# First norm and first projection of a hybrid encoder step: GpSimd's share moved to VectorE, smaller token tiles, a half-block projection loop and another queue for the first weights

## The chip, the core and the metric

The kernel runs on one core of a Trainium2 chip, in one launch. The metric is the device time of that launch in microseconds (us). The kernel before was timed three times: 3157.12, 3160.59 and 3160.79 us, a median of 3160.59 us.

## The reference

One layer of a streaming encoder works on a prompt of 2048 tokens and on a sample of 32 tokens, each token a vector of 1024 channels, in float32. The layer has an attention branch, a gated linear attention branch (GLA), a merge, and a gated MLP with a short convolution. The change sits in its very first lines:

```python
def rmsnorm(x, g):
    xf = x.astype(jnp.float32)
    r = lax.rsqrt(jnp.mean(xf * xf, axis=-1, keepdims=True) + EPS)
    return (xf * r).astype(x.dtype) * g
...
    shift_m, scale_m, gate_m, shift_f, scale_f, gate_f = adaln_modulation(c, p['w_ada'], p['b_ada'])

    h = rmsnorm(x, p['g_pre_mix']) * (1.0 + scale_m) + shift_m
    z = h @ p['w_in']
```

Here `adaln_modulation` is a small product of the conditioning vector with `w_ada`. The matrix `w_in` has 5136 columns. The part that matters here makes `h` for all 2080 tokens and the 512 columns of `z` that hold GLA's queries ("Q") and keys ("K").

## The kernel before

**Layout.** Channels lie on the partitions: the 1024 channels are 8 chunks of 128 (index `k`), and tokens run along the free axis. The 2080 tokens are 5 blocks of 416 (`NB`), and each block is two half blocks of 208 (`NH`), numbered 0 to 9. Each float32 operand of a large product is split into a high and a low part of type float32r. A product then takes three matmuls (`mm3`, L78 to L80): high by high, high by low, low by high. `h` lives in `hA` (blocks 0 to 3) and `hB` (block 4), a high and a low tile each.

**The steps of the first norm**, for one half block `hb`:

- `prep_load` (L263): two DMAs (L267) on the queue of SyncE (SP), each bringing a tile of 4 chunks by 208 tokens. Six such tiles exist, three half blocks' worth.
- `prep_stats` (L270): ScalarE squares two chunks at a time (L276, L279), and another engine adds the squares up (L280, L281). The adding engine is VectorE for half blocks 0 and 1 and GpSimd for 2 to 9. One buffer holds the squares that wait to be added.
- `rstd_bcast` (L140): the sums are split (L69 on ScalarE, L72 on VectorE). TensorE adds them over the partitions with a matrix of ones (L148, L149). ScalarE takes logarithm and exponential (L154, L155), and VectorE polishes the result in three dependent steps (L156 to L158). This is the reciprocal root `r`, on all partitions.
- `prep_apply` (L290), per chunk: VectorE multiplies by `r` and the scale (L299), ScalarE adds the shift and rounds to the high part (L300), VectorE takes the low part (L301). Half block 2 is an exception: for its odd chunks GpSimd does the multiplications (L288, L297).

**The conditioning** (`ada_load` L305, `ada` L314): 8 small products whose weights come in DMAs of 256 KB (L310) through six buffers, again on SP's queue. The scale and shift of two chunks are ready after a second set of tiny matmuls (L327) and VectorE's L134 and L138.

**The projection** (`wave` L341): 4 column chunks of 128 (two of Q, two of K) each accumulate over the 8 chunks `k` in a PSUM bank. One step of `k` is 4 x 3 = 12 matmuls of 416 columns, and one block is 96 matmuls. Its weights are loaded in pieces (`w_pieces`, L180): a DMA of 256 KB on SP's queue (L187) into one of two raw buffers, ScalarE's rounding (L191), VectorE's low part (L192). After a block, `t_evac` (L202) copies the banks out, Q on ScalarE (L230) and K on VectorE (L233), and stores them (L235).

**Order.** TensorE's instructions run in the order of the program text. The instructions of the other engines, and SP's DMAs, are reordered at build time by a list scheduler that follows data dependences and the text's order as priority; on the chip each queue then runs strictly in the built order. Block 0 is written out by hand (L353 to L418), interleaved with the conditioning. Blocks 1 to 4 are the loop at L422 over `s_` = 2 to 9. Two values of `s_` make one block: the first takes `k` = 0 to 3 of all 416 tokens, the second `k` = 4 to 7. In step `s_` the kernel loads half block `s_` + 4, takes statistics of `s_` + 3, and finishes and applies the norm of `s_` + 2. In block 4 the two steps are Q's chunks and K's chunks instead.

**PSUM.** Of 8 banks, `psx` (tag `px`) has 6 and `psm` (tag `pm`) has 2. The waves, the conditioning and the norm's sums all use `px` here.

**After it** comes `n_tile`, the projection of the other columns, which starts as soon as block 4 is done.

Of the kernel before, what the change touches and what calls it, by code (L numbers as in the profile page):

```python
# [10 lines left out]
F32 = mybir.dt.float32  # L11
# [3 lines left out]
OP = mybir.AluOpType  # L15
# [43 lines left out]
def encoder_step(ctx: ExitStack, tc: tile.TileContext, I, O):  # L59
# [120 lines left out]
    def w_pieces(wp, c0, n, w, kp, wr=2):  # L180

        hi = wp.tile([128, KD, w], F32R, name="wh", tag="wh")
        lo = wp.tile([128, KD, w], F32R, name="wl", tag="wl")

        def piece(kk):
            raw = wp.tile([128, kp, w], F32, name="wr", tag="wr", bufs=wr)
            d = nc.sync.dma_start(raw[:, :, :n], dap(w_in, kk * 128 * WIN + c0, [[WIN, 128], [128 * WIN, kp], [1, n]]))  # L187
            if behind.pop():
                tc.keep_in_program_order(d)
            behind.append(False)  # L190
            nc.scalar.activation(hi[:, kk:kk + kp, :n], raw[:, :, :n], AF.Copy)  # L191
            nc.vector.tensor_sub(lo[:, kk:kk + kp, :n], raw[:, :, :n], f32(hi[:, kk:kk + kp, :n]))  # L192

        return (hi, lo), [lambda kk=kk: piece(kk) for kk in range(0, KD, kp)]
# [48 lines left out]
    with ExitStack() as st:  # L243
# [17 lines left out]
        POOL = {2: (1, 3, 5, 7)}  # L261

        def prep_load(hb, q_=nc.sync):  # L263
            XK[hb] = []
            for k in range(0, KD, 4):
                x = pp.tile([128, 4, NH], F32, name="xk", tag="xk", bufs=6)
                q_.dma_start(x, dap(I["xT"], k * 128 * T + NH * hb, [[T, 128], [128 * T, 4], [1, NH]]))  # L267
                XK[hb].append(x)

        def prep_stats(hb, add):  # L270

            sq = pp.tile([128, 2, NH], F32, name="sq", tag="sq", bufs=2)
            for k in range(0, KD, 2):
                x = XK[hb][k // 4][:, k % 4:k % 4 + 2]
                if k == 0:
                    nc.scalar.activation(sq, x, AF.Square)  # L276
                    continue
                s2 = pp.tile([128, 2, NH], F32, name="sq2", tag="sq2")
                nc.scalar.activation(s2, x, AF.Square)  # L279
                add.tensor_add(sq, sq, s2)  # L280
            add.tensor_add(sq[:, 0], sq[:, 0], sq[:, 1])  # L281
            return lambda: rstd_bcast(pp, psx, "px", sq[:, 0], NH, NH, 2)

        def prep_scale(hb):
            for k in POOL.get(hb, ()):
                for a, e, s in parts(NH * hb, NH):
                    xs = XK[hb][k // 4][:, k % 4, a:e]
                    nc.gpsimd.tensor_scalar(xs, xs, mod[:, 1, k, s:s + 1], 1.0, op0=OP.mult, op1=OP.mult)  # L288

        def prep_apply(hb, r, ks_=range(KD)):  # L290
            for k in ks_:
                for a, e, s in parts(NH * hb, NH):
                    hi, lo = [h_at(x, k, NH * hb + a, e - a) for x in range(2)]
                    xs = XK[hb][k // 4][:, k % 4, a:e]
                    s1, s2 = mod[:, 1, k, s:s + 1], mod[:, 0, k, s:s + 1]
                    if k in POOL.get(hb, ()):
                        nc.gpsimd.tensor_mul(xs, xs, r[:, a:e])  # L297
                    else:
                        nc.vector.scalar_tensor_tensor(xs, xs, s1, r[:, a:e], op0=OP.mult, op1=OP.mult)  # L299
# [39 lines left out]
        w0, steps = zip(*[w_pieces(wp, c0, 256, 272, 2, 2) for _, c0 in first])  # L339

        def wave(b, ks_, ps, chunks=range(4)):  # L341
            for k in ks_:
                for i in chunks:
                    mm3(ps[i][:, :NB], [t_terms(w0[i // 2], 128 * (i % 2), b, k)], first=k == 0, last=k == KD - 1)
# [8 lines left out]
        fin0 = prep_stats(0, nc.vector)()  # L353
# [6 lines left out]
        fin1 = prep_stats(1, nc.vector)()  # L360
# [8 lines left out]
        prep_load(2)  # L369
# [6 lines left out]
        prep_load(3)  # L376
# [5 lines left out]
        fins[2] = prep_stats(2, nc.gpsimd)  # L382
# [5 lines left out]
        prep_load(4)  # L388
# [5 lines left out]
        fins[3] = prep_stats(3, nc.gpsimd)  # L394
# [7 lines left out]
        prep_scale(2)  # L402
        m1 = ada(3, 0)
        r2 = fins.pop(2)()()
# [4 lines left out]
        prep_apply(2, r2)  # L409
        prep_load(5)  # L410
        wave(0, (5, ), ps)
        f3 = fins.pop(3)()
        wave(0, (6, ), ps)
        r3 = f3()
        wave(0, (7, ), ps)
        prep_apply(3, r3)
        fins[4] = prep_stats(4, nc.gpsimd)
# [1919 lines left out]
```

## Time and profile before

| what | before |
|---|---|
| median of three timed runs | 3160.59 us |
| the profiled execution, its own time | 3162.02 us |
| its span (first to last instruction) | 3160.3 us |
| first matmul of the projection of block 0 starts at | 27.21 us |
| block 1 starts at | 71.25 us |
| block 2 starts at | 97.36 us |
| block 3 starts at | 121.72 us |
| block 4 starts at | 145.75 us |
| the next stage's first matmul (`n_tile`) starts at | 163.85 us |

A row of the timeline reads: start, duration, engine, line, operation, output <- inputs, shapes, count, and in brackets the idle time before it with what released it. PE is TensorE, PEld its weight load, DVE VectorE, ACT ScalarE, POOL GpSimd, SP the queue of SyncE. Matmuls are pipelined, so the spacing of their starts tells the rate, not their durations. A row of the waits reads: who waited, for whom, total us, times, longest. A row of groups reads: line, engine, operation, tiles and shapes, count, busy us, mean ns, and the idle time before with its releasers. Stretches list, per engine, busy us and number of instructions.

### The profile page before, as it was taken

The numbers are of one execution on the slowest core, as the hardware profiler recorded it, in microseconds if no ns is written. First come the engines' busy times: TensorE is split into PE (matmuls) and PEld (weight loads), VectorE is DVE, ScalarE is ACT, GpSimd is POOL, SyncE is SP. The second block draws the span as 40 slices with busy tenths as digits, with TensorE's granted clock in tenths as the row PEclk, the third lists the DMA queues.
The fourth block names the chain that finished last, engine by engine and source line by source line (L and its number), as shares of the span: only waits on it lengthen the run. The fifth ranks groups of instructions, "written<-read, shape, count | busy, mean of one in ns | idle before, by whom it ended". The sixth has DMA issues, their size and how long they took to land. (4 is left out here: it accounts for less than half of the span.)

```text
span 3160.3 us, 56426 instructions
## 1 busy us (share of the span) xinstructions
PE 3047.7 (96%) x19748; PEld 2947.7 (93%) x19748; DVE 2239.8 (71%) x4879; ACT 1648.8 (52%) x3792; POOL 269.4 (9%) x427
## 2 busy tenths in 40 slices
PE   6999999999999999999999999999999999999997
PEld 4899999998999999988999899999999999999997
DVE  6735617774555555566677799998888778897877
ACT  4522224443555555544454655567666556576755
POOL 2201201112111111120000000000000000000001
PEclk9999999999999999999999999999999999999998
DMA  7354435554433334575457686788897667888784
GB/s 220 91 156 125 139 98 142 137 137 128 130 109 111 107 100 117 169 230 184 140 175 227 211 256 210 223 256 225 249 265 217 189 189 230 263 250 284 242 267 146
DMA packets 598478, 580.12 MB, mean 184 GB/s; under 512 B 53201, under 2 KB 526530, under 8 KB 598194
## 3 DMA queue, kind: packets, MB, share of 16 engines
q1 hardware_dynamic: 553026, 527.86, 56.2%
q10 hardware_dynamic: 44432, 47.34, 4.7%
q8 instruction: 155, 2.54, 0.3%
q0 software_dynamic: 736, 1.33, 0.2%
q14 instruction: 129, 1.06, 0.1%
HBM read 388.71 MB, written 187.65 MB: 182 GB/s over the span
## 5 line engine op out<-in xcount | busy, mean ns | idle before, releaser
L1882 PE MATMUL ad<-hA,hB 128*128 128x350 f32 (+2 forms) x1734 | 301.7, 324 | 3.8 <-DVE hB L1824 2.4
L1882 PEld LDWEIGHTS ad<-hA,hB 128*128 128x128 f32 x1734 | 282.5, 189 | 5.5 <-DVE hB L1824 3.3
L78 PE MATMUL pm<-hA,wh 128*128 128x416 f32 x768 | 287.4, 374 | 0.0
L79 PE MATMUL pm<-hA,wh 128*128 128x416 f32 x768 | 269.3, 351 | 0.0
L80 PE MATMUL pm<-hA,wl 128*128 128x416 f32 x768 | 269.3, 351 | 0.0
L1824 DVE TENSOR_TENSOR hA<-raws,hA 128x512 fp32r<-128x512 f32 (+1 forms) x367 | 241.9, 668 | 13.0 <-ACT hA L1819 12.7
L1819 ACT ACTIVATE hA<-raws 128x512 fp32r<-128x512 f32 (+1 forms) x367 | 222.0, 617 | 29.9 <-DMA raws<-in_w_up_dram 11.1
L1882 PE MATMUL ad<-hA,hA 128*128 128x348 f32 (+2 forms) x1308 | 225.5, 323 | 2.5 <-ACT work L2008 1.8
L1882 PE MATMUL g<-hA,hB 128*128 128x348 f32 (+2 forms) x1248 | 217.1, 323 | 6.4 <-ACT work L2004 3.5
L1882 PEld LDWEIGHTS ad<-hA,hA 128*128 128x128 f32 x1308 | 211.8, 188 | 3.9 <-ACT work L2008 2.4
L1882 PEld LDWEIGHTS g<-hA,hB 128*128 128x128 f32 x1248 | 202.3, 188 | 9.1 <-ACT work L2004 4.7
L1882 PE MATMUL ad<-hA 128*128 128x350 f32 (+2 forms) x1173 | 205.1, 324 | 4.2 <-DVE hA L1734 4.1
L1882 PEld LDWEIGHTS ad<-hA 128*128 128x128 f32 x1173 | 191.7, 190 | 5.0 <-DVE hA L1734 4.4
L1824 DVE TENSOR_TENSOR hB<-raws,hB 128x512 fp32r<-128x512 f32 (+1 forms) x289 | 190.9, 668 | 6.5 <-ACT hB L1819 6.1
L1819 ACT ACTIVATE hB<-raws 128x512 fp32r<-128x512 f32 (+1 forms) x289 | 175.8, 617 | 25.3 <-DMA raws<-in_w_up_dram 11.8
L69 ACT ACTIVATE pth<-pp 128x256 fp32r<-128x256 f32 (+1 forms) x288 | 106.4, 373 | 139.2 <-PE pp L1027 135.9
L72 DVE TENSOR_TENSOR ptl<-pp,pth 128x256 fp32r<-128x256 f32 (+1 forms) x288 | 118.1, 414 | 85.2 <-ACT pth L69 82.4
L78 PE MATMUL pn<-wh,hA 128*128 128x256 f32 (+1 forms) x624 | 176.9, 283 | 0.0
L79 PE MATMUL pn<-wl,hA 128*128 128x256 f32 (+1 forms) x624 | 176.3, 283 | 0.0
L80 PE MATMUL pn<-wh,hA 128*128 128x256 f32 (+1 forms) x624 | 176.1, 282 | 0.0
L1991 ACT COPY g<-ad 128x348 f32<-128x348 f32 (+2 forms) x102 | 44.3, 434 | 244.1 <-PE ad L1882 156.4
L1882 PE MATMUL g<-hA,hA 128*128 128x350 f32 (+2 forms) x894 | 157.4, 325 | 4.0 <-ACT g L1991 2.3
(507 smaller groups left out, 8468.6 us busy)
## 6 DMA issues: line engine op xcount, KB each, us to landing
raws<-in_w_up_dram SPq DMA_DIRECT2D x220, 256.0 KB, 4.3
raws<-sW SPq DMA_DIRECT2D x176, 256.0 KB, 3.8
sW<-raws SPq DMA_DIRECT2D x88, 256.0 KB, 3.6
raws<-in_w_down_dram SPq DMA_DIRECT2D x80, 256.0 KB, 5.2
wr<-in_w_in_dram SPq DMA_DIRECT2D x76, 256.0 KB, 3.2
sgT<-tx ACTq DMA_DIRECT2D x80, 208.0 KB, 1.9
wa<-in_w_ada_dram SPq DMA_DIRECT2D x64, 256.0 KB, 3.0
keys<-ks SPq DMA_DIRECT2D x128, 128.0 KB, 2.9
```

The costliest lines, as they stand in the source:

```text
L69: i = nc.scalar.activation(hi, src, AF.Copy)
L72: nc.vector.tensor_sub(lo, src, f32(hi))
L78: nc.tensor.matmul(out, ah, bh, start=first and i == 0, stop=False)
L79: nc.tensor.matmul(out, ah, bl, start=False, stop=False)
L80: nc.tensor.matmul(out, al, bh, start=False, stop=last and i == n - 1)
L1819: act = nc.scalar.activation(hi[:, :n], raw(i, n), AF.Copy)
L1824: nc.vector.tensor_sub(lo[:, :n], raw(i, n), f32(hi[:, :n]))
L1882: nc.tensor.matmul(out[:, :w], l_[:, k], r_[:, k, :w], start=first and k == 0 and i == 0, stop=k == n - 1 and i == 2, skip_group_check=True)
L1991: nc.scalar.copy(g[:, 0, :w], ad[:, 0, :w])
```

## The change

- All GpSimd work of the first norm goes: `POOL`, `prep_scale` and the argument that chose the adding engine are removed. VectorE adds all squares and multiplies all chunks.
- Token tiles have 2 chunks instead of 4 and there are 12 instead of 6: the same memory, twice the DMAs.
- The norm's sums over the partitions use the two banks of `psm` instead of `px`.
- Blocks 1 to 4 are projected by half blocks: `wave` takes a column offset `a` and a width `n`, and one step `s_` takes all 8 `k` of one half block in matmuls of 208 columns. Block 0 keeps 416 columns.
- With it the order shifts: step `s_` loads half block `s_` + 3, finishes and applies `s_` + 1, and takes statistics of `s_` + 2. In the hand-written part of block 0 half block 3 is no longer applied, and loads and statistics move.
- The 8 DMAs of the first weights (L187) are issued from GpSimd's queue instead of SP's.

```diff
-    def w_pieces(wp, c0, n, w, kp, wr=2):
+    def w_pieces(wp, c0, n, w, kp, wr=2, q_=nc.sync):
...
-            d = nc.sync.dma_start(raw[:, :, :n], dap(w_in, kk * 128 * WIN + c0, [[WIN, 128], [128 * WIN, kp], [1, n]]))
+            d = q_.dma_start(raw[:, :, :n], dap(w_in, kk * 128 * WIN + c0, [[WIN, 128], [128 * WIN, kp], [1, n]]))
...
-        POOL = {2: (1, 3, 5, 7)}
...
-            for k in range(0, KD, 4):
-                x = pp.tile([128, 4, NH], F32, name="xk", tag="xk", bufs=6)
-                q_.dma_start(x, dap(I["xT"], k * 128 * T + NH * hb, [[T, 128], [128 * T, 4], [1, NH]]))
+            for k in range(0, KD, 2):
+                x = pp.tile([128, 2, NH], F32, name="xk", tag="xk", bufs=12)
+                q_.dma_start(x, dap(I["xT"], k * 128 * T + NH * hb, [[T, 128], [128 * T, 2], [1, NH]]))
...
-                add.tensor_add(sq, sq, s2)
-            add.tensor_add(sq[:, 0], sq[:, 0], sq[:, 1])
-            return lambda: rstd_bcast(pp, psx, "px", sq[:, 0], NH, NH, 2)
+                nc.vector.tensor_add(sq, sq, s2)
+            nc.vector.tensor_add(sq[:, 0], sq[:, 0], sq[:, 1])
+            return lambda: rstd_bcast(pp, psm, "pm", sq[:, 0], NH, NH, 2)
...
-                    if k in POOL.get(hb, ()):
-                        nc.gpsimd.tensor_mul(xs, xs, r[:, a:e])
-                    else:
-                        nc.vector.scalar_tensor_tensor(xs, xs, s1, r[:, a:e], op0=OP.mult, op1=OP.mult)
+                    nc.vector.scalar_tensor_tensor(xs, xs, s1, r[:, a:e], op0=OP.mult, op1=OP.mult)
...
-        w0, steps = zip(*[w_pieces(wp, c0, 256, 272, 2, 2) for _, c0 in first])
+        w0, steps = zip(*[w_pieces(wp, c0, 256, 272, 2, 2, nc.gpsimd) for _, c0 in first])
...
-        def wave(b, ks_, ps, chunks=range(4)):
+        def wave(b, ks_, ps, chunks=range(4), a=0, n=NB):
...
-                    mm3(ps[i][:, :NB], [t_terms(w0[i // 2], 128 * (i % 2), b, k)], first=k == 0, last=k == KD - 1)
+                    wh, wl, hh, hl = t_terms(w0[i // 2], 128 * (i % 2), b, k)
+                    mm3(ps[i][:, a:a + n], [(wh, wl, hh[:, a:a + n], hl[:, a:a + n])], first=k == 0, last=k == KD - 1)
...
-        prep_apply(2, r2)
-        prep_load(5)
+        f2 = fins.pop(2)()
         wave(0, (5, ), ps)
-        f3 = fins.pop(3)()
-        wave(0, (6, ), ps)
-        r3 = f3()
-        wave(0, (7, ), ps)
-        prep_apply(3, r3)
-        fins[4] = prep_stats(4, nc.gpsimd)
+        prep_load(4)
+        r = f2()
+        prep_apply(2, r)
+        fins[3] = prep_stats(3)
+        wave(0, (6, 7), ps)
         wave_evac(0, ps)
...
+        f1 = fins.pop(3)()
         for s_ in range(2, 10):
-            b = s_ // 2
-            if s_ + 4 < 10:
-                prep_load(s_ + 4)
+            b, a = s_ // 2, NH * (s_ % 2)
+            if a == 0:
+                ps = wave_tiles()
             if s_ + 3 < 10:
-                fins[s_ + 3] = prep_stats(s_ + 3, nc.gpsimd)
-            k0 = 4 * (s_ % 2)
-            if s_ + 2 < 10:
-                fin = fins.pop(s_ + 2)()
-            if s_ % 2 == 0:
-                ps = wave_tiles()
-            if b < 4:
-                wave(b, range(k0, k0 + 1), ps)
-                prep_apply(s_ + 2, fin())
-                wave(b, range(k0 + 1, k0 + 4), ps)
-            elif s_ % 2 == 0:
-
-                wave(b, range(KD), ps, (0, 1))
-                wn = load_w(wp, 2048, 256, 272, 2, 2)
+                prep_load(s_ + 3)
+            if s_ < 8:
+                wave(b, (0, 1), ps, a=a, n=NH)
+                prep_apply(s_ + 1, f1())
+                if s_ + 2 < 10:
+                    fins[s_ + 2] = prep_stats(s_ + 2)
+                    f1 = fins.pop(s_ + 2)()
+                wave(b, range(2, 6), ps, a=a, n=NH)
+                if s_ == 7:
+                    prep_apply(9, f1())
+                wave(b, (6, 7), ps, a=a, n=NH)
             else:
-                wave(b, range(KD), ps, (2, 3))
+                for a in (0, NH):
+                    wave(b, range(KD), ps, (0, 1) if s_ == 8 else (2, 3), a=a, n=NH)
+                if s_ == 8:
+                    wn = load_w(wp, 2048, 256, 272, 2, 2)
```

More of the change, by code (lines that the diff above doesn't have):

```diff
@@ L260, in encoder_step, with prep_stats @@
         XK = {}
-        POOL = {2: (1, 3, 5, 7)}
         def prep_load(hb, q_=nc.sync):
             XK[hb] = []
-            for k in range(0, KD, 4):
-                x = pp.tile([128, 4, NH], F32, name="xk", tag="xk", bufs=6)
-                q_.dma_start(x, dap(I["xT"], k * 128 * T + NH * hb, [[T, 128], [128 * T, 4], [1, NH]]))
+            for k in range(0, KD, 2):
+                x = pp.tile([128, 2, NH], F32, name="xk", tag="xk", bufs=12)
+                q_.dma_start(x, dap(I["xT"], k * 128 * T + NH * hb, [[T, 128], [128 * T, 2], [1, NH]]))
                 XK[hb].append(x)
-        def prep_stats(hb, add):
+        def prep_stats(hb):
             sq = pp.tile([128, 2, NH], F32, name="sq", tag="sq", bufs=2)
             for k in range(0, KD, 2):
-                x = XK[hb][k // 4][:, k % 4:k % 4 + 2]
+                x = XK[hb][k // 2]
                 if k == 0:
@@ L279, in prep_stats @@
                 nc.scalar.activation(s2, x, AF.Square)
-                add.tensor_add(sq, sq, s2)
-            add.tensor_add(sq[:, 0], sq[:, 0], sq[:, 1])
-            return lambda: rstd_bcast(pp, psx, "px", sq[:, 0], NH, NH, 2)
[L284 to L288, printed above, removed]
+                nc.vector.tensor_add(sq, sq, s2)
+            nc.vector.tensor_add(sq[:, 0], sq[:, 0], sq[:, 1])
+            return lambda: rstd_bcast(pp, psm, "pm", sq[:, 0], NH, NH, 2)
         def prep_apply(hb, r, ks_=range(KD)):
@@ L293, in prep_apply @@
                     hi, lo = [h_at(x, k, NH * hb + a, e - a) for x in range(2)]
-                    xs = XK[hb][k // 4][:, k % 4, a:e]
+                    xs = XK[hb][k // 2][:, k % 2, a:e]
                     s1, s2 = mod[:, 1, k, s:s + 1], mod[:, 0, k, s:s + 1]
-                    if k in POOL.get(hb, ()):
-                        nc.gpsimd.tensor_mul(xs, xs, r[:, a:e])
-                    else:
-                        nc.vector.scalar_tensor_tensor(xs, xs, s1, r[:, a:e], op0=OP.mult, op1=OP.mult)
+                    nc.vector.scalar_tensor_tensor(xs, xs, s1, r[:, a:e], op0=OP.mult, op1=OP.mult)
                     nc.scalar.activation(hi, xs, AF.Identity, bias=s2)
@@ L351, in wave_evac @@
                 t_evac(stg, first[i // 2][0], i % 2, b, ps[i][:, :NB])
-        fin0 = prep_stats(0, nc.vector)()
+        fin0 = prep_stats(0)()
         ada_load(1, 1)
@@ L359, in encoder_step @@
         r0 = fin0()
-        fin1 = prep_stats(1, nc.vector)()
+        fin1 = prep_stats(1)()
         m1 = ada(0, 0)
@@ L368, in encoder_step @@
         ada_load(2, 1)
-        prep_load(2)
         m0 = ada(1, 1)
@@ L375, in encoder_step @@
         ada_load(3, 1)
-        prep_load(3)
+        prep_load(2)
         prep_apply(0, r0, [0, 1])
@@ L381, in encoder_step @@
         ada_load(3, 0)
-        fins[2] = prep_stats(2, nc.gpsimd)
+        prep_load(3)
+        fins[2] = prep_stats(2)
         wave(0, (0, ), ps)
@@ L387, in encoder_step @@
         prep_apply(1, r1, [2, 3])
-        prep_load(4)
         for s_ in steps:
@@ L393, in encoder_step @@
         m1 = ada(2, 0)
-        fins[3] = prep_stats(3, nc.gpsimd)
         wave(0, (2, ), ps)
@@ L401, in encoder_step @@
         m0()
-        prep_scale(2)
         m1 = ada(3, 0)
-        r2 = fins.pop(2)()()
         wave(0, (4, ), ps)
```

## The prediction

> **What bounds the kernel now.** The page's head gives the span; the profiled execution took 3162.0 us, so 1.7 us lie around it.
>
> ```profile
> span 3160.3 us, 56426 instructions
> ```
>
> Next I cut the span into stretches at the first matmul of each block (busy us and count per engine, then granted clock). The order of rows: block 0 with the gap behind it, blocks 1, 2, 3, 4, and the rest from 203 us on.
>
> ```profile
> 27.20:71.25 44.05, 33.30 (x186) 27.10 (x186) 31.05 (x67) 20.25 (x47) 17.31 (x20) 0.88 0.70 214
> 71.25:97.35 26.10, 22.70 (x100) 21.14 (x101) 20.60 (x46) 14.74 (x36) 13.28 (x11) 0.80 0.31 90
> 97.35:121.70 24.35, 19.99 (x101) 18.07 (x100) 18.50 (x42) 13.18 (x33) 8.00 (x9) 1.00 0.37 108
> 121.70:145.75 24.05, 21.24 (x102) 19.72 (x101) 19.18 (x57) 11.95 (x32) 2.18 (x4) 0.93 0.12 37
> 145.75:163.85 18.10, 18.10 (x97) 17.96 (x97) 13.63 (x36) 6.03 (x15) 0.00 (x0) 1.00 0.63 205
> 203.00:3146.00 2943.00, 2884.29 (x18809) 2803.96 (x18808) 2091.82 (x4539) 1563.53 (x3593) 217.79 (x369) 1.00 0.62 185
> ```
>
> The last row: TensorE is busy 2884 of 2943 us, so whatever the first stage saves or loses goes straight to the end. Block 4 needs 18.1 us and waits for nothing; blocks 1 to 3, the same 96 matmuls, take 26.1 + 24.35 + 24.05 = 74.5 us. The recoverable part is there and in block 0. TensorE's waits between 27 and 164 us say for whom:
>
> ```profile
> PE px L78 <- ACT hA L300: 5.1, 2, 3.0
> PE px L78 <- ACT tx L230: 4.1, 4, 1.6
> PE px L79 <- DVE hA L301: 3.7, 4, 1.7
> ```
>
> It waits for normed tokens and for emptied banks (`tx`). Behind both stand VectorE and ScalarE, as the groups of 0 to 165 us show:
>
> ```profile
> L299 DVE SCALAR_TENSOR_TENSOR xk<-xk,mod,rstd 128x208 f32<-128x208 f32 x68 | 35.0, 558 | 0.4
> L280 POOL TENSOR_TENSOR sq<-sq,sq 128x416 f32<-128x416 f32 x24 | 29.9, 1246 | 40.0 <-ACT sq L279 39.8
> ...
> L276 ACT ACTIVATE sq<-xk 128x416 f32<-128x416 f32 x10 | 5.5, 545 | 11.5 <-DMA xk<-in_xT_dram 11.4
> ...
> L156 DVE SCALAR_TENSOR_TENSOR rstt<-pst,rst 128x208 f32<-128x208 f32 x10 | 3.7, 370 | 11.3 <-ACT rst L155 11.3
> ...
> L280 DVE TENSOR_TENSOR sq<-sq,sq 128x416 f32<-128x416 f32 x6 | 3.6, 593 | 4.5 <-ACT sq L279 4.5
> ```
>
> Two things to see. VectorE idles 11.3 us for `rst` (L155); on ScalarE that step is queued behind squares (L276) that wait for token DMAs. And GpSimd's additions (1.25 us against 0.59 on VectorE) go with slower VectorE instructions: L299 averages 558 ns, though its median is 426 and its worst 1261, as its tokens' view says. Undisturbed, three take 1.12 us, one every 0.35 us:
>
> ```profile
> L299 DVE SCALAR_TENSOR_TENSOR xk<-xk,mod,rstd x84: 244/426/1261, 20.4 to 148.6; 128x208 f32<-128x208 f32 x68, 128x176 f32<-128x176 f32 x8, 128x32 f32<-128x32 f32 x8
> ```
>
> ```profile
> 133.62 1.12 DVE L299 SCALAR_TENSOR_TENSOR xk<-xk,mod,rstd 128x208 f32<-128x208 f32 x3
> ```
>
> **The change part by part.** *Squares and multiplications to VectorE.* Added per half block from 2 on: three additions of 0.59 and a shorter one, which I put between zero and 0.59 at 0.37 like other 208-column operations (L156): 2.1 us. Removed: GpSimd's disturbance, (558 - 426) ns x 68 = 9 us for L299 alone, about 1 us per half block. So VectorE's work rises by about 1 us per half: 16 apply operations at 0.35 make 5.6, squares 2.1, the split and three steps on `r` 4 x 0.37 = 1.5, K's copy at about 0.6: **9.8 us per half block**.
>
> *Tiles and order.* Loads become twice as many. Statistics of half block `s_` + 2 use tokens that were asked for one step earlier, into buffers that are free by then, so the token wait in front of L276 should go, and with it most of the 11.3 us before L156. What is late next is VectorE itself, which also has one half block less of lead.
>
> *Half-block matmuls.* The width of 208 exists in the sums of the norm:
>
> ```profile
> 90.39 0.26 PE L148 MATMUL pst<-sh,ones 128*128 128x208 f32 x1
> 90.49 0.27 PE L149 MATMUL pst<-sl,ones 128*128 128x208 f32 x1
> 90.60 0.36 PE L78 MATMUL px<-hA,wh 128*128 128x416 f32 x1
> ```
>
> Starts are 0.10 and 0.11 us apart; I take 0.105. A 416-column matmul costs (163.66 - 145.75) / 95 = 0.1885:
>
> ```profile
> 145.75 0.35 PE L78 MATMUL px<-hB,wh 128*128 128x416 f32 x1
> ...
> 163.66 0.35 PE L80 MATMUL px<-hB,wl 128*128 128x416 f32 x1
> ```
>
> A block becomes 192 x 0.105 = 20.2 us where it was 18.1. Hence **block 4: +2.1 us** (0.10 gives +1.1, 0.11 gives +3.0). The Trainium skill speaks against narrow matmuls: "TensorE: Matmul & The Clock Gate" says, under "The mechanism", that a weight load overlaps running matmuls only when it targets other rows of the array; with the 107 ns that its section "LDWEIGHTS (loading the stationary operand)" gives for 128 columns, block 4 would by estimate take 192 x (0.105 + 0.107) = 41 us. The trace disagrees: both 208-column matmuls load weights into all 128 rows and still start 0.10 us apart, so this rule gets no chance below.
>
> *Blocks 1 to 3.* A half block takes TensorE 96 x 0.105 + 0.2 = 10.3 us, VectorE 9.8, and now takes 74.5 / 6 = 12.4. TensorE cannot go below 10.3; VectorE at 9.8 with the full present wait (11.3 us over 5 waits, 2.3 each) needs 12.1, and with waits for emptied banks (4.1 us over 4) about 13. I take 11.0, nearest to the engines' own work because what held ScalarE goes. **6 x 11.0 = 66: -8.5 us** (62 to 78, that is -12.5 to +3.5). Half block 9, mixed from prompt and sample, has 16 more VectorE operations of at least 0.24 us (its tokens' view), 3.9 us, and its statistics come right behind the apply of half block 8; half of that should show: **+2 us** (0 to +5).
>
> *Block 0: GpSimd's part.* Its squares of half block 2 made VectorE wait in order, and TensorE behind it:
>
> ```profile
> 40.91 0.62 POOL L281 TENSOR_TENSOR sq<-sq 128x208 f32<-128x208 f32 x1
> ```
>
> ```profile
> 41.97 0.38 DVE L72 TENSOR_TENSOR sl<-sq,sh 128x208 fp32r<-128x208 f32 x1 [2.12 <-ACT sh L69]
> ```
>
> ```profile
> 42.73 0.81 PE L327 MATMUL pm<-sel,mr 128*128 128x2 f32 x4 [1.74 <-DVE mr L323]
> ```
>
> *Block 0: weights.* A raw buffer came free at 30.3 us (L192 ends), but SP, in order behind conditioning weights and tokens, issued the next pair at 36.56, the last four from 51.78. The last rounding waited for them at 55.58, VectorE behind it reached the shift (L134) only at 58.39, and TensorE stood at chunk 6:
>
> ```profile
> 29.65 0.69 DVE L192 TENSOR_TENSOR wl<-wr,wh 128x512 fp32r<-128x512 f32 x1 [0.75 <-ACT wh L191]
> ```
>
> ```profile
> 36.56 2.16 SPq L187 DMA_DIRECT2D wr<-in_w_in_dram  x2
> ...
> 51.78 6.39 SPq L187 DMA_DIRECT2D wr<-in_w_in_dram  x4
> ```
>
> ```profile
> 55.58 0.63 ACT L191 ACTIVATE wh<-wr 128x512 fp32r<-128x512 f32 x1 [5.22 <-DMA wr<-in_w_in_dram]
> ```
>
> ```profile
> 58.39 0.15 DVE L134 TENSOR_TENSOR mod<-pm,bada 128x4 f32<-128x4 f32 x1
> ```
>
> ```profile
> 59.82 0.53 PE L78 MATMUL px<-hA,wh 128*128 128x416 f32 x1 [2.97 <-ACT hA L300]
> 62.03 0.71 PE L79 MATMUL px<-hA,wh 128*128 128x416 f32 x1 [1.67 <-DVE hA L301]
> 62.54 0.55 PE L80 MATMUL px<-hA,wl 128*128 128x416 f32 x1
> 62.89 0.55 PE L78 MATMUL px<-hA,wh 128*128 128x416 f32 x1
> ```
>
> Alone on GpSimd's queue a piece is asked for when its buffer is free, some 6 us earlier. What is queued behind such a wait on GpSimd is only the next piece. The named stalls are 1.74 + 2.97 + 1.67 = 6.4 us; behind them matmuls start 0.35 apart instead of 0.19, about 13 of them, 2 us more; and block 1 no longer needs half block 3 applied before it starts (16 operations x 0.35 = 5.6 us of VectorE's work moved behind it). Against this VectorE gets two statistics (4.2) and half block 2's four odd multiplications (1.4) in block 0. Together 14.0 - 5.6 = 8.4, and some relief from GpSimd's disturbance: **-9 us** (0 if something else is as late, -14 with nothing late).
>
> *Start.* The weights' DMAs, with their size and median time to landing:
>
> ```profile
> wr<-in_w_in_dram SPq DMA_DIRECT2D x76, 256.0 KB, 3.2
> ```
>
> On a queue of their own the first ones may now compete with the first tokens: two pieces of 256 KB ahead of them at block 0's 214 GB/s are 2.4 us, while smaller first tiles land earlier. **0** (-2 to +3). The later stages: 0.
>
> **Sum.** -8.5 + 2 + 2.1 - 9 = -13.4; 3162.0 - 13.4 = 3148.6 for a profiled execution. The median of the timed runs is 1.4 below the profiled one: **3147 us**.
>
> **The rivals.** *Nothing measurable.* VectorE's extra additions and lost lead eat the waits that go: halves at 12.4 (0), block 4 and half block 9 at +4.1, block 0 at -4, half of its named stalls: 3161 us. For it speaks that VectorE was busy 58.3 of 74.5 us in blocks 1 to 3 already; against it, that its idle time had a named releaser which goes.
>
> *The queue brings nothing in block 0.* The two raw buffers stay two; if they, and not SP's order, set the pace, block 0 gives only GpSimd's 1.74 and the moved apply less the additions, about -2: -8.5 + 4.1 - 2 = -6.4, 3154 us. "DMA: Bandwidth & Descriptors" of the Trainium skill, under "Issuing engines are not separate DMA queues", says that other queues save only issue time; the trace disagrees, since the pair issued at 36.56 had a buffer from 30.3.
>
> *All stalls gone.* TensorE sets the pace: 6 x 10.3 (-12.7), block 4 +2.1, block 0 -14: 3136 us.
>
> *Slower: the one half block of lead is too short.* Then each half is a closed chain: sums and `r` (0.2 + 2 x 0.4 on ScalarE + 1.1), apply 5.6, squares in turns with ScalarE through the one buffer (4 x 0.55 + 2.1), split 0.7, copy 0.6, 1 us of handing over: 14.3 us; TensorE, idle a third of it, drops to the slow spacing (half of 0.35 per matmul: 96 x 0.175 = 16.8). Between them 15.5 x 6 = 93 (+18.5), +4.1, -9: +13.6, 3174 us. It decides from (74.5 + 6.3 + 9 - 4.1) / 6 = 14.3 us per half. For it: block 1 had a granted clock of 0.80; against: the squares depend only on tokens that lie ready, and fill VectorE's waits.
>
> **How the numbers follow.** Forecast 0.52, queue brings nothing 0.15, all stalls gone 0.08, nothing measurable 0.12, slower 0.13. A change of 0.2% (6.3 us) is about what can be measured here. Faster by more: 0.52 + 0.08 + half of the queue's case = 0.68; slower 0.13; the rest 0.19. The range reaches from 3135 (all stalls gone) to 3161 (above it the slower case and a little of the unchanged one).
>
> **What would show it.** Right: block 0's first matmul to block 1's near 35 us; matmuls of 208 columns 0.105 apart; halves of 11 us; `rst` waits below 5 us; no GpSimd additions; a first `n_tile` matmul near 150 us. Wrong: TensorE waiting for L300 or L301 in every half, a slow clock throughout blocks 1 to 3, or weights still late at chunk 6.

## The result, and the profile after

The changed kernel takes **3185.68 us** (median of five runs, 3183.89 to 3192.24) against 3160.59 us for the kernel before in five runs of the same session: a ratio of 1.0086, 95% interval 1.0075 to 1.0097. It is 25 us slower where the forecast had it 13.6 us faster. The profiled execution has a span of 3183.1 us, 22.8 more than before. The head of its page, and the span cut at the first matmul of each block as before (busy us and count of PE, PEld, DVE, ACT, POOL, then the granted clock; blocks 0 to 4):

```profile
span 3183.1 us, 57247 instructions
```

```profile
30.30:57.22 26.92, 26.92 (x183) 23.70 (x183) 21.36 (x61) 14.16 (x34) 1.23 (x3) 1.00 0.74 230
57.22:81.94 24.72, 22.64 (x197) 22.20 (x197) 21.05 (x57) 13.99 (x34) 0.00 (x0) 1.00 0.35 105
81.94:113.63 31.69, 25.10 (x199) 24.71 (x197) 22.53 (x61) 15.54 (x37) 0.00 (x0) 0.84 0.31 92
113.63:143.95 30.32, 24.49 (x200) 23.96 (x199) 19.59 (x53) 12.88 (x31) 0.00 (x0) 0.94 0.17 49
143.95:165.40 21.45, 21.45 (x194) 21.42 (x192) 15.78 (x51) 6.03 (x18) 0.00 (x0) 1.00 0.42 134
```

Block 0 takes 26.9 us instead of 44.05 and waits for nothing. It starts 3.1 us later. Blocks 1 to 3 take 86.7 us instead of 74.5, block 4 21.5 instead of 18.1. All in all the first stage ends at 165.5, 1.7 us later than before: up to here the change is worth nothing, either way. The loss follows. TensorE's waits in the first 220 us name it:

```profile
PE pn L79 <- DVE wl L192: 14.8, 1, 14.8
PE px L78 <- ACT tx L230: 10.4, 3, 6.6
PE pn L78 <- ACT wh L191: 8.4, 2, 7.6
```

The first and third row lie behind block 4. `pn` is the next stage, `n_tile`, and it waits 7.6 and then 14.8 us for its first weights (timeline of TensorE):

```profile
173.11 0.58 PE L78 MATMUL pn<-wh,hA 128*128 128x256 f32 x1 [7.56 <-ACT wh L191]
188.53 0.58 PE L79 MATMUL pn<-wl,hA 128*128 128x256 f32 x1 [14.83 <-DVE wl L192]
```

What stands ahead of the weights stands on three queues. ScalarE's timeline, first before, then after, shows the first wait:

```profile
154.85 0.62 ACT L191 ACTIVATE wh<-wr 128x512 fp32r<-128x512 f32 x1
...
173.85 1.04 ACT L69 ACTIVATE acch<-acc 128x1024 fp32r<-128x1024 f32 x1
```

```profile
170.57 1.06 ACT L69 ACTIVATE acch<-acc 128x1024 fp32r<-128x1024 f32 x1 [19.04 <-DVE acc L477]
171.53 0.50 ACT L230 ACTIVATE tx<-px 128x416 f32<-128x416 f32 x1
...
172.43 1.15 ACT L191 ACTIVATE wh<-wr 128x512 fp32r<-128x512 f32 x2 [0.40 <-ACT tx L230]
```

`acch` is the rounding of the late modulation (`mod_late`), side work of the next stages. Before, it came after the weights. Now ScalarE waits 19 us for its operand, and behind it stand block 4's evacuation (L230) and the rounding of the weights' first pieces (L191), which SP had asked for at 46 us. VectorE's timeline, before and after, shows the second wait, the weights' low part (L192): before behind 4 of the late modulation's multiplications, after behind 31, many of which wait for their DMA:

```profile
155.50 1.29 DVE L192 TENSOR_TENSOR wl<-wr,wh 128x512 fp32r<-128x512 f32 x2
```

```profile
187.12 0.75 DVE L477 SCALAR_TENSOR_TENSOR acc<-wa,sc,acc 128x512 f32<-128x512 f32 x1 [0.21 <-DMA wa<-in_w_ada_dram]
187.79 1.29 DVE L192 TENSOR_TENSOR wl<-wr,wh 128x512 fp32r<-128x512 f32 x2
```

And SP's DMAs, first before, then after (`wa` are here the late modulation's tiles, `wr` the weights' next two pieces):

```profile
146.10 9.68 SPq L486 DMA_DIRECT2D wa<-in_w_ada_dram  x4
156.22 0.98 SPq L187 DMA_DIRECT2D wr<-in_w_in_dram  x2
```

```profile
146.47 40.79 SPq L472 DMA_DIRECT2D wa<-in_w_ada_dram  x17
188.50 0.98 SPq L187 DMA_DIRECT2D wr<-in_w_in_dram  x2
```

Before, four loads of side work stand ahead of these two pieces; after, seventeen, and each waits in order for one of two buffers to come free. These two pieces are not the ones that TensorE waits for, which were asked for at 46 us. They also need the raw buffers that VectorE's L192 empties: both times SP issues them within 0.1 us of the end of its first piece (156.2 and 188.5 us). So SP's order delays the first weights only through the side work that it feeds to the two engines. No edit of the change touches these lines. The list scheduler, given another first stage, built another order for the queues.

### The profile page after: what moved, and what is told of

Read it like the earlier page. It is cut to its first block, busy times and chain, and to the rows that moved or that the text cites. A ratio compares the mean times of both kernels' runs of the same rounds, so it can differ in the third digit from the quotient of the medians.

```text
span 3183.1 us, 57247 instructions
## 1 busy us (share of the span) xinstructions
PE 3056.9 (96%) x20132; PEld 2963.4 (93%) x20132; DVE 2240.9 (70%) x4915; ACT 1650.3 (52%) x3792; POOL 235.3 (7%) x395
## 5 line engine op out<-in xcount | busy, mean ns | idle before, releaser
L1810 DVE TENSOR_TENSOR hA<-raws,hA 128x512 fp32r<-128x512 f32 (+1 forms) x367 | 242.3, 669 | 12.4 <-ACT hA L1805 12.2
L79 PE MATMUL pn<-wl,hA 128*128 128x256 f32 (+1 forms) x624 | 178.2, 286 | 15.0 <-DVE wl L192 14.8
L72 DVE TENSOR_TENSOR ptl<-pp,pth 128x256 fp32r<-128x256 f32 (+1 forms) x288 | 118.1, 414 | 84.1 <-ACT pth L69 81.6
```

The lines of the kernel that those rows point to most:

```text
L72: nc.vector.tensor_sub(lo, src, f32(hi))
L79: nc.tensor.matmul(out, ah, bl, start=False, stop=False)
L1810: nc.vector.tensor_sub(lo[:, :n], raw(i, n), f32(hi[:, :n]))
```

## The experiments

**Theory and rival.** The theory: the loss is the built order behind block 4. The first rival: the loss is the stages' own work (narrow matmuls, lost lead), and the waits behind block 4 would turn up elsewhere. Each run is timed against the kernel before in its own session; its median there was 3162.66 us for the first four runs below, 3161.39 for the next four, 3163.31 for the three after, 3161.30 for the last three. The starts (us, from the traces), gathered here for all runs; `pw` is the first matmul of the late modulation, early in the next stage:

| kernel | block 0 | block 1 | block 4 | n_tile | pw | median | ratio (95%) |
|---|---|---|---|---|---|---|---|
| before | 27.2 | 71.3 | 145.8 | 163.9 | 244.1 | 3160.59 | |
| after | 30.3 | 57.2 | 144.0 | 173.1 | 269.7 | 3185.68 | 1.0086 (1.0075-1.0097) |
| two queues held | 30.2 | 57.4 | 144.1 | 165.5, waits at 175 | 268.2 | 3191.22 | 1.0086 (1.0066-1.0106) |
| block 4 wide | 30.2 | 57.2 | 144.8 | 163.3 | 246.7 | 3169.50 | 1.0020 (1.0011-1.0030) |
| weights on SP | 25.2 | 58.0 | 146.0 | 175.6 | 272.4 | 3190.80 | 1.0086 (1.0071-1.0101) |
| evacuation first | 30.0 | 57.0 | 142.6 | 173.4 | 274.7 | 3194.14 | 1.0093 (1.0078-1.0109) |
| three queues held | 30.2 | 58.1 | 145.7 | 167.1 | 247.5 | 3165.42 | 1.0012 (1.0003-1.0020) |
| Q chunks first, 6 | 30.1 | 57.4 | 142.7 | 161.3 | 244.2 | 3164.31 | 1.0009 (1.0000-1.0018) |
| before, block 4 narrow | 25.9 | 70.8 | 145.6 | 170.3 | 264.3 | 3184.04 | 1.0071 (1.0055-1.0088) |
| before, queue alone | 40.1 | 74.7 | 149.7 | 167.8 | 249.7 | 3169.23 | 1.0026 (1.0016-1.0036) |
| Q first, GpSimd adds | 30.1 | 61.3 | 154.0 | 172.8 | 253.2 | 3175.19 | 1.0042 (1.0028-1.0055) |
| before, no GpSimd | 25.9 | 66.6 | 135.8 | 153.9 | 234.9 | 3153.95 | 0.9971 (0.9961-0.9981) |
| Q chunks first, 8 | 30.5 | 57.4 | 143.8 | 161.9 | 244.3 | 3164.81 | 1.0006 (0.9997-1.0015) |
| half blocks undone | 30.0 | 68.3 | 129.8 | 147.9 | 231.6 | 3147.04 | 0.9953 (0.9941-0.9966) |
| the same, weights on SP | 25.7 | 68.1 | 131.9 | 150.0 | 231.4 | 3150.42 | 0.9961 (0.9949-0.9974) |
| two halves' lead, narrow | 30.5 | 63.7 | 146.7 | 167.4 | 255.8 | 3177.38 | 1.0051 (1.0036-1.0067) |

**Two queues held.** The changed kernel, with the late modulation's loads on SP and its roundings on ScalarE held behind the last of the next stage's first weights:

```diff
-                nc.sync.dma_start(w, I["w_ada"][128 * k:128 * k + 128, 512 * blk:512 * blk + 512])
+                with tc.issue_after(wn_d):
+                    nc.sync.dma_start(w, I["w_ada"][128 * k:128 * k + 128, 512 * blk:512 * blk + 512])
...
-            split(ah, al, acc)
+            with tc.issue_after(wn_a):
+                split(ah, al, acc)
```

> The changed kernel, with the first weights of the next stage (its L187 DMAs and L191 roundings) kept ahead, on SP's and ScalarE's queues, of the side work that the list scheduler had put before them (17 loads of the late conditioning, one large rounding). Theory A: the loss comes from that built order alone, so the three waits of the next stage's matmuls (7.6 + 14.8 + 0.9 us) and some slow-clock matmuls behind them go: 3185.7 - 24 = 3162 us, and the next stage's first matmul, at 173.1 us now, comes at about 165.6. Rival B: the half-block projection is what is slower, and the weights are late only because everything is: no more than 5 us come back, 3181 us or above.

The next stage starts at 165.5 without a wait for weights, and then stands still (timeline of TensorE, then of VectorE):

```profile
195.84 0.58 PE L78 MATMUL pn<-wh,hA 128*128 128x256 f32 x1 [20.75 <-DVE tx L236]
```

```profile
194.53 0.75 DVE L482 SCALAR_TENSOR_TENSOR acc<-wa,sc,acc 128x512 f32<-128x512 f32 x1 [1.17 <-DMA wa<-in_w_ada_dram]
195.20 1.08 DVE L236 COPY tx<-px 128x416 f32<-128x416 f32 x2
```

It wants a PSUM bank that block 4's K columns still hold. Their copy (L236 there) stands on VectorE behind 29 multiplications of side work, most of which wait for a DMA. So the same overtaking sits on a third queue, and mending two moves the wait: 20.8 us in place of 22.4. By itself this run spoke for the rival.

**Block 4 wide.** The changed kernel with block 4 in 416 columns:

```diff
-                for a in (0, NH):
-                    wave(b, range(KD), ps, (0, 1) if s_ == 8 else (2, 3), a=a, n=NH)
+                wave(b, range(KD), ps, (0, 1) if s_ == 8 else (2, 3))
```

> The changed kernel with block 4 alone projected in matmuls of 416 columns again. Theory A: twice as many matmuls in block 4 make the scheduler count on a later end of that block, and so it fits side work in front of the weights; with the old width the weights come first again (in the built order they do), so the 23 us of waits go and block 4 shrinks from 21.4 to 18.1: 3185.7 - 23 - 3 = 3159 us. Rival B: only the matmuls' own price comes back, 3 us: 3182 us.

The next stage starts at 163.3 with no wait for weights: SP has four loads of side work ahead of them again. In its session it is 6.8 us above the kernel before, so 18 of the 25 us are gone, though block 4's matmuls themselves are worth only 3. That lies between what theory and rival had said; where the other 7 us arise was not settled (in the trace `pw` comes 2.6 us later than before). One line brings the order back, so the order follows block 4's instructions; which property of them tips it was not looked at.

**First weights back on SP.** The changed kernel without its change of queue:

```diff
-        w0, steps = zip(*[w_pieces(wp, c0, 256, 272, 2, 2, nc.gpsimd) for _, c0 in first])
+        w0, steps = zip(*[w_pieces(wp, c0, 256, 272, 2, 2) for _, c0 in first])
```

> The changed kernel with the first weights back on SP's queue. Block 0 took 26.9 us in the changed kernel against 44.1 before. Theory A: the queue gave most of that, so block 0 takes 9 us longer again, the late weights come as late behind it: 3195 us. Rival C: the queue gave nothing, GpSimd's absence did it all: 3186 us as now.

Block 0 starts 5.1 us earlier and lasts 5.9 us longer; block 1 starts 0.8 us later and the time is the same within the intervals. So the queue shifts where block 0 waits; it is neither the loss nor the reason that block 1 starts 14 us earlier than before.

**Evacuation first.** In the changed kernel, Q's evacuation ahead of the second half of the next apply and ahead of the squares on ScalarE:

```diff
+                    wave_evac(b, ps)
+                    with tc.issue_after(last_q[0]):
+                        prep_apply(s_ + 1, r, range(4, KD))
+                        fins[s_ + 2] = prep_stats(s_ + 2)
+                        f1 = fins.pop(s_ + 2)()
```

> The changed kernel with the bank copies of each block put, on ScalarE's queue, ahead of the second half of the next apply and of the next squares (whose place in the text moves behind the copies; half block 9 is applied after the first half of block 4's Q chunks). Theory A: TensorE's 10.4 us of waits for emptied banks and the slow clock behind them go, and block 4 ends some 10 us earlier, but the next stage's weights are held by the side work, not by TensorE, so the total stays within 5 us: 3181 to 3186 us. Rival D: the waits for banks are part of the loss, and the total falls with them, to 3173 us.

The waits for banks in blocks 1 to 3 are gone, and those for the sums of squares (`pst` <- `sh`) rise to 17.1 us between 20 and 220 us, where 3.2 of them lay before: one wait for another, and blocks 1 to 3 take 85.6 us. The time is above what either side had said. Half block 9, now applied inside block 4, makes TensorE wait there (3.3 us for its first tile), and the stage ends at 173.4 instead of 165.5. Then the next stage waits 12.5 us for block 4's K copy behind side work on VectorE, as with two queues held.

**Three queues held.** As the first run, with VectorE's first multiplication of the side work held too, behind the weights and block 4's last K copy:

```diff
-                        nc.vector.tensor_scalar(acc[:, s], w, sc[:, k, s:s + 1], None, op0=OP.mult)
+                        with tc.issue_after(wn_v), tc.issue_after(last_k[0]):
+                            nc.vector.tensor_scalar(acc[:, s], w, sc[:, k, s:s + 1], None, op0=OP.mult)
```

> The changed kernel with the late modulation's first work held back on all three queues: its loads on SyncE and its rounding on ScalarE behind the first weights of the next stage, as before, and its first multiplication on VectorE behind the last of these weights and behind block 4's last K evacuation. Theory (the built order lets side work overtake what TensorE needs next; the loss is that): no wait of the next stage's first matmuls over 2 us in the first 220 us, that stage starting near 165.5, and 3161 to 3166 us: the changed kernel's 3185.7 less most of the 22.4 us of its two waits. Rival (the side work must be done by a due time in any case, and is only waited for elsewhere, as with two queues mended): 3180 or more, with a wait of over 10 us somewhere between 165 and 300 us.

The theory came true but for a start 1.6 us later than it said: 3165.42 us, and in the first 320 us no wait for weights or K copies is left (the `pb` row is the side work's own):

```profile
PE px L78 <- ACT tx L234: 9.7, 2, 6.5
PE pst L149 <- DVE sl L72: 3.7, 2, 2.0
PE pb L463 <- DMA tr<-in_rel_rev_dram: 3.5, 3, 1.6
```

The first stage is written as in the changed kernel and takes 1.6 us more; the order of three queues alone is worth 21 us (25 above the kernel before, now 4). The rival falls. Whether holding VectorE alone would do was not run.

**The kernel before with block 4 narrow.** The converse: nothing of the change but two halves of 208 columns in block 4.

```diff
-                wave(b, range(KD), ps, (0, 1))
+                for a in (0, NH):
+                    wave(b, range(KD), ps, (0, 1), a=a, n=NH)
```

> The kernel before with nothing changed but block 4's matmuls, in two halves of 208 columns. Theory (more instructions in block 4 shift the built order of the side work): loads of the late modulation and its rounding stand ahead of the next stage's weights, TensorE waits over 15 us for these weights behind block 4, and the time is 3176 to 3186 us. Rival (the overtaking comes from the other parts, and a narrow block 4 costs its own matmuls alone): 3161 to 3165 us, no wait for weights over 2 us.

3184.04 us, nearly the whole loss from one edit, by the same mechanism (waits of TensorE between 20 and 320 us, and SP):

```profile
PE pn L79 <- DVE wl L192: 11.1, 1, 11.1
...
PE pn L78 <- ACT wh L191: 4.5, 2, 3.2
```

```profile
145.91 35.60 SPq L489 DMA_DIRECT2D wa<-in_w_ada_dram  x16
181.78 0.98 SPq L187 DMA_DIRECT2D wr<-in_w_in_dram  x2
```

**The kernel before with the queue alone changed**, as in the change's diff.

> The kernel before with nothing changed but the queue of the first weights. Theory (before, block 0 waits for applied tiles and statistics, and weights only once, 1.3 us): block 0 within 2 us of its 44.0 us, and 3158 to 3163 us. Rival (the bytes in front of the x tiles on the one queue set block 0): block 0 shorter by 5 us or more, and 3150 to 3157 us, if the later stages follow.

Block 0 is shorter by 9.5 us, as the rival had it, and the kernel is slower by 8, as neither had it. The first projection matmul comes 13 us later:

```profile
40.14 0.71 PE L78 MATMUL px<-hA,wh 128*128 128x416 f32 x1 [6.56 <-ACT hA L300]
```

The DMA view of the first 41 us (issues with KB each and median time to landing), of this kernel and then of the kernel before:

```profile
wa<-in_w_ada_dram SPq DMA_DIRECT2D x14, 512.0 KB, 7.7
xk<-in_xT_dram SPq DMA_DIRECT2D x6, 416.0 KB, 8.9
wr<-in_w_in_dram POOLq DMA_DIRECT2D x8, 256.0 KB, 6.2
```

```profile
wa<-in_w_ada_dram SPq DMA_DIRECT2D x16, 512.0 KB, 7.8
xk<-in_xT_dram SPq DMA_DIRECT2D x8, 416.0 KB, 7.8
wr<-in_w_in_dram SPq DMA_DIRECT2D x6, 256.0 KB, 7.6
```

All eight pieces of weights move in that time, and two loads of the conditioning and two of tokens fewer. That fits weights which, on a queue of their own, go ahead of bytes that are wanted first; no run separates this from other reasons. The next stage starts 4 us late.

**Q chunks first.** Block 4 wide, and in the first half of blocks 1 to 3 the Q chunks' matmuls for six `k` ahead of the K chunks':

```diff
+                    wave(b, range(6), ps, (0, 1), n=NH)
...
+                    wave(b, range(6), ps, (2, 3), n=NH)
```

> The changed kernel with block 4 in 416 columns, and in the first half of blocks 1 to 3 the matmuls of the Q chunks for six of the eight input chunks ahead of those of the K chunks, so that the second pair of PSUM banks is wanted about 4 us later. Theory (the 10.3 us of waits for ScalarE's Q evacuations are a matter of which matmuls come first): those waits under 3 us in sum, the next stage starting near 156 to 158, and 3160 to 3164 us. Rival (the time goes to the statistics and the applied tiles instead, as when the evacuations were put first): the next stage starting at 162 to 164 as with block 4 wide alone, and 3168 to 3171 us.

In between: the waits for Q's evacuations halve to 5.4 us and the stage ends 2 us earlier than with block 4 wide alone. **For all eight `k`:**

> The version with block 4 in 416 columns, with the Q chunks ahead for all eight input chunks in place of six. Theory (the 5.4 us of waits for ScalarE's Q evacuations go, but VectorE's 11.4 us per half block then set the pace): the waits for evacuations under 1 us, the next stage starting no more than 2 us earlier than 161.3, 3161 to 3165 us. Rival (the waits were the pace): the next stage starting at 156 or earlier, 3156 to 3160 us.

Two waits of 2.2 us stay, which the theory had at nothing; the stage ends no earlier and the time is as it said: so these waits are not the pace.

**GpSimd's additions back.** The version with six `k` first, with the squares of half blocks 2 to 9 added on GpSimd:

```diff
+            add = nc.vector if hb < 2 else nc.gpsimd
...
-                nc.vector.tensor_add(sq, sq, s2)
+                add.tensor_add(sq, sq, s2)
```

> The version with block 4 in 416 columns and the Q chunks first, with the additions of squares of half blocks 2 to 9 back on GpSimd. Theory (taking GpSimd out is a wash: it gives VectorE 2.1 us more per half block, three additions of 591 ns and one of 375 ns, and saves it about 0.1 us on each of the 16 applying operations, 530 against 423 ns and 496 against 430 ns): applying operations back near 0.5 us, blocks 1 to 3 within 2 us of the 85.2 us that they took in that version, and 3161 to 3167 us. Rival 1 (VectorE's 11.4 us per half block set blocks 1 to 3 and the additions are its surplus): blocks 1 to 3 shorter by 6 us or more, 3156 to 3160. Rival 2 (GpSimd's 1.3 us additions lengthen the chain of statistics, which a lead of one half block can't hide): longer by 4 us or more, 3168 or above.

Rival 2 came true: blocks 1 to 3 take 92.7 us against 85.2, the time rises by about 9 us (12 above the kernel before instead of 3). VectorE's low parts (L293) average 0.44 us, not the 0.5 that the theory expected, for only 2 of the 48 run while GpSimd does. ScalarE waits for GpSimd's additions instead:

```profile
ACT sq L280 <- POOL sq L281: 11.8, 10, 1.2
```

**The kernel before without GpSimd.** Nothing but its work given to VectorE:

```diff
-        POOL = {2: (1, 3, 5, 7)}
+        POOL = {}
...
-                fins[s_ + 3] = prep_stats(s_ + 3, nc.gpsimd)
+                fins[s_ + 3] = prep_stats(s_ + 3, nc.vector)
```

> The kernel before with nothing changed but GpSimd's work, all of it given to VectorE. Theory (block 0 before waited for statistics and applied tiles that GpSimd made late, and slowed VectorE while it ran): block 0 shorter than 44.0 us by 5 us or more, blocks 1 to 3 within 3 us of their 74.5 us, 3150 to 3158 us. Rival (VectorE is the pace before too, and the relief lay in the order and in the smaller tiles): block 0 within 3 us of 44, blocks 1 to 3 longer, 3161 to 3170. Should the built order shift as with block 4 narrow, loads of the late modulation stand ahead of the next stage's weights, TensorE waits over 8 us for them and the time is above 3175.

3153.95 us, 9 us faster, as the theory said, but from another place: block 0 gains only 3.3 us, while blocks 1 to 3 take 69.2 instead of 74.5. The groups between 57 and 145 us, of the kernel before and of this one:

```profile
L299 DVE SCALAR_TENSOR_TENSOR xk<-xk,mod,rstd 128x208 f32<-128x208 f32 (+2 forms) x61 | 29.5, 530 | 0.3
...
L280 POOL TENSOR_TENSOR sq<-sq,sq 128x416 f32<-128x416 f32 x18 | 23.0, 1278 | 34.3 <-ACT sq L279 34.2
```

```profile
L299 DVE SCALAR_TENSOR_TENSOR xk<-xk,mod,rstd 128x208 f32<-128x208 f32 (+1 forms) x69 | 24.7, 403 | 0.1
...
L280 DVE TENSOR_TENSOR sq<-sq,sq 128x416 f32<-128x416 f32 x18 | 10.6, 588 | 5.6 <-ACT sq L279 4.6 <-ACT sq L276 0.8
```

The addition costs 588 ns on VectorE against 1278 on GpSimd, and VectorE's applying multiplication averages 403 instead of 530 ns. The Trainium skill says both in "GPSIMD Engine Reference": "4.1 Engine selection" calls GpSimd about two times slower for such operations, and "1. Specifications" says that it shares its SBUF interfaces with VectorE. The rows agree. In the kernel before, between 57 and 145 us, the 23 multiplications of 208 columns that overlap a GpSimd instruction in time average 739 ns, the other 29 average 426. With GpSimd's additions back in the changed order, hardly any overlap and hardly any slow down; so the price depends on what runs at the same moment.

**Half blocks undone.** The changed kernel with blocks 1 to 4 in 416 columns and tiles applied two half blocks ahead, as before; tiles, engines and queue stay as changed:

```diff
-            b, a = s_ // 2, NH * (s_ % 2)
...
+            b = s_ // 2
...
+            k0 = 4 * (s_ % 2)
...
-                wave(b, (0, 1), ps, a=a, n=NH)
-                prep_apply(s_ + 1, f1())
...
+                wave(b, range(k0, k0 + 1), ps)
+                prep_apply(s_ + 2, fin())
+                wave(b, range(k0 + 1, k0 + 4), ps)
```

> The changed kernel with one part undone: blocks 1 to 4 in 416 columns, applied tiles two half blocks ahead as before; no GpSimd, two-chunk tiles and the weights' queue stay. Theory (the half blocks are the loss: more matmul instructions, evacuations that the next block's banks wait for, and the built order behind; taking GpSimd out is the gain): block 0 as in the changed kernel, block 1 from about 66, blocks 1 to 3 in 69 to 72 us, block 4 18.1, next stage from 153 to 156 with no wait for its weights over 2 us, and 3151 to 3157 us. Rival (the tiles or the queue carry a loss of their own): blocks 1 to 3 over 75 us or the next stage after 160, and 3161 or above.

**3147.04 us, the fastest of all runs**, 14 us below the kernel before and below the theory's range: blocks 1 to 3 take 61.5 us where it said 69 to 72. (Block 0, counted to the start of block 1, is longer than in the changed kernel, because half block 3 is applied in it again.) **With the first weights back on SP as well:**

> The same, and the first weights back on SyncE's queue, so that half blocks and queue are both undone. Theory (the queue only shifts where block 0 waits: it starts about 5 us earlier and lasts as much longer): first projection matmul near 25, block 1 within 2 us of its start in the version with the queue changed, and a time within 3 us of it. Rival (with the early loads crowded the later start is a cost that stays): 4 us or more faster.

Block 0 starts 4.3 us earlier, block 1 at the same time. The medians lie 3.4 us apart and their intervals overlap, so the two cannot be told apart.

**Two halves' lead, narrow.** The fastest version with 208 columns by half blocks in blocks 1 to 3 again, block 4 still wide:

```diff
-                wave(b, range(k0, k0 + 1), ps)
+                wave(b, (0, 1), ps, a=a, n=NH)
...
-                wave(b, range(k0 + 1, k0 + 4), ps)
+                wave(b, range(2, KD), ps, a=a, n=NH)
```

> The version with half blocks undone, with blocks 1 to 3 in 208 columns again by half blocks, but applied tiles still two half blocks ahead and block 4 in 416 columns. Theory (narrow matmuls and the banks' evacuations slow blocks 1 to 3, not the lead of one half block): blocks 1 to 3 8 us or more longer than with 416 columns, with waits for ScalarE's Q evacuations of 5 us or more. Rival (VectorE's 11.4 us per half block is the pace and a lead of two hides the rest): within 3 us of them. The built order may shift here as well (more instructions in blocks 1 to 3): then the next stage waits over 5 us for its weights and the time is above 3165.

Blocks 1 to 3 in three versions, one row each (changed; half blocks undone; narrow with the longer lead):

```profile
57.22:143.95 86.73, 72.23 (x591) 70.88 (x591) 63.17 (x167) 42.41 (x101) 0.00 (x0) 0.92 0.27 81
```

```profile
68.28:129.80 61.52, 58.47 (x301) 56.88 (x301) 55.30 (x158) 38.19 (x94) 0.00 (x0) 0.97 0.31 88
```

```profile
63.68:146.69 83.01, 74.95 (x589) 74.17 (x589) 62.44 (x174) 42.83 (x105) 0.00 (x0) 0.88 0.27 78
```

Wide, TensorE is busy 58.5 and VectorE 55.3 of 61.5 us: both are nearly full. Narrow, with the same lead, the blocks take 21.5 us more (16 counted from the first projection matmul, since block 1 started earlier). And with the longer lead the narrow form reaches block 4 no sooner than the changed kernel (116 us from the first projection matmul against 114). So the narrow form is the cost (its matmuls and the order built with them, which this run does not separate), not the short lead. The theory's reason holds only in part: the waits for Q's evacuations are 3.3 us, not 5. The next stage again waits for its weights (7.6 us), as was said could happen.

## Why the prediction was wrong

**The step that failed: "The later stages: 0."** It rested on the sentence that "whatever the first stage saves or loses goes straight to the end". TensorE is indeed the bound from 203 us on, and what is late at `pw` is late at the end (25.6 us there, 22.8 in the span). But between block 4 and that point lies work that the built order mixes with side work. The two waits there, 7.6 + 14.8 us, are nearly the whole result. Holding three queues takes them away (3165), and block 4's width alone brings such waits into the kernel before (3184). No rival of the prediction named the built order, so no chance stood on it. Of its signs of being wrong none came: TensorE waits 0.4 us for applied tiles, the granted clock is 1.00, 0.84 and 0.94 in blocks 1 to 3, and no weights are late in block 0. All three looked at the first stage alone.

**Blocks 1 to 3: "6 x 11.0 = 66: -8.5 us"** also failed: 86.7 us, +12.2. That is 14.45 us per half block, just over the 14.3 from which the slow rival was to decide (it gave +18.5 here). Part of its closed chain is visible in VectorE's waits between 57 and 145 us, changed kernel and half blocks undone:

```profile
DVE sq L279 <- ACT sq L278: 9.4, 14, 0.9
DVE rstt L156 <- ACT rst L155: 7.6, 4, 3.9
```

```profile
DVE rstt L156 <- ACT rst L155: 1.5, 1, 1.5
...
DVE sq L279 <- ACT sq L278: 0.5, 2, 0.4
```

The prediction held against that rival that the squares "fill VectorE's waits". In the changed kernel they don't: VectorE adds one, idles for ScalarE's next, and has no apply to do in between. In the wide version additions, polishing and applying alternate: VectorE idles 6.2 of its 61.5 us there (waits of 2.8 us for the first two squares, L275, are part of it), against 23.6 of 86.7 in the changed kernel. By itself the narrow matmul adds 3 x (192 x 0.112 - 18.1) = 10 us to TensorE's work, at the measured spacing. The gain that the forecast saw did not come with it: to waits and slow clock TensorE loses about as much time as before (86.7 - 64.5 = 22.2 us against 74.5 - 54.3 = 20.2). How much of that is the built order of VectorE and ScalarE, and how much the place of the sums on TensorE behind narrow matmuls, was not separated.

**Block 4: +2.1** measured +3.4. The kind was right, the spacing was not: 21.45 / 192 = 0.112 us, beyond the two starts on which 0.105 rested. That still leaves no room for the 41 us weighed from the Trainium skill. Its page "TensorE: Matmul & The Clock Gate" also admits, under "The mechanism", a load into a background buffer of weights, which the forecast left out; it fits the trace, where weight loads are busy 21.42 of block 4's 21.45 us beside the matmuls.

**Block 0: -9** measured -17.1, beyond its bound of -14. A later start shortens block 0, so the two terms belong together: -14.0 here, -13.2 with the weights on SP. The named stalls all went. The queue was not the reason: with the weights on SP block 1 starts within 1 us. With GpSimd's work taken out and nothing else changed, block 0 still takes 40.7 us. What does most is that half block 3 no longer has to be applied before block 1: with the half blocks undone, and it applied there again, block 1 starts at 68.3, 11 us later; TensorE waits there 1.7 and 3.3 us for the sums of half block 3 and 4.9 us for its first tile. 5.6 us were given for it.

**Start: 0** measured +3.1, just past its bound: the first weights do compete with the first tokens (on SP's queue the start is 25.2). **Squares to VectorE:** right. It is busy 63.2 / 6 = 10.5 us per half block against 9.8 estimated, and taking GpSimd out is the one part that was seen to gain by itself. **Half block 9: +2** came out, as far as one wait can show it. Its sums are the last in the stage, and their low part (L72) stands on VectorE behind operations of half block 8's apply, as the forecast had it; the 2.0 us lie in block 3:

```profile
141.07 0.36 PE L149 MATMUL pst<-sl,ones 128*128 128x208 f32 x1 [2.00 <-DVE sl L72]
```

Without the later stages the sum is -17.1 + 3.1 + 12.2 + 3.4 = +1.6 us. That is as little as the rival called nothing measurable had, but by chance: two large terms of opposite sign, not its small ones. Nearly all of the 23 us is the order behind it.

## What to carry to other kernels

Where a scheduler builds the queues' order, an edit's price includes the order of everything near it: compare the built order of each queue before and after, around the next stage's first loads, before trusting a sum of durations. When side work overtakes, look at every queue that the waiting work passes; holding two of three moved a wait of some 20 us and gained nothing. Split a bundled change: here taking GpSimd out gained 9 us by itself, the half blocks lost more than that, and leaving them out made the fastest kernel.

## What the runs showed of the hardware

Matmuls of 208 columns start 0.11 us apart, and twice as far apart after a pause (changed kernel, behind the wait in block 2):

```profile
89.36 0.54 PE L78 MATMUL px<-hA,wh 128*128 128x208 f32 x1 [6.59 <-ACT tx L230]
...
91.05 0.41 PE L78 MATMUL px<-hA,wh 128*128 128x208 f32 x1
91.26 0.41 PE L79 MATMUL px<-hA,wh 128*128 128x208 f32 x1
...
95.31 0.28 PE L78 MATMUL px<-hA,wh 128*128 128x208 f32 x1
95.43 0.27 PE L79 MATMUL px<-hA,wh 128*128 128x208 f32 x1
```

The granted clock (the third number from the end) of the two stretches is the same story:

```profile
89.36:95.26 5.90, 5.90 (x26) 5.69 (x27) 1.73 (x4) 0.70 (x2) 0.00 (x0) 0.50 0.31 111
95.26:97.30 2.04, 2.04 (x20) 2.04 (x20) 1.25 (x4) 0.69 (x3) 0.00 (x0) 0.99 0.29 104
```

After 6.6 us of idling the spacing is 0.21 us for 5.9 us, then 0.11 again: about 3 us on top of the wait. Behind the wait of 3.5 us in block 3, half the clock came only 1.2 us after the restart and lasted 3.4 us (119.2 to 122.6). "TensorE: Matmul & The Clock Gate" of the Trainium skill, under "What's actually happening", has the clock halve after at least one idle window of about 3.4 us and return after at least one busy one, with windows that run freely. The halving agrees; the return took 1.7 such windows the first time and about one the second.
